# A hybrid decoder layer on one core: VectorE order in W_down, weight parts kept in DRAM, transpose banks, an early norm and one split moved

## The chip, the cores and the metric

The kernel runs on one core of one Trainium2 chip. The metric is the time of one execution on the device in microseconds. A profiled execution is slower or faster than the timed ones by some tenths of a per cent; where times inside an execution are compared, they come from the profiled one.

## What is computed

The layer takes x (1, 1024, 1024) in float32. Cut to what matters:

```python
h = rms_norm(x, norm_mix_pre)
proj = h @ w_in                                   # 1024 x 2568: u, v, z, xBC, dt
u_a, v_a, z_b, xbc_b, dt_b = split(proj)
y_a = gmlp_mixer(u_a, v_a, ...)                   # gelu, layer norm of v, causal 128 x 128 mixing per head
y_b = mamba2_mixer(z_b, xbc_b, dt_b, ...)         # conv of 4 taps, silu, chunked scan, silu gate, group norm
x = x + rms_norm(concat(y_a, y_b) @ w_out, norm_mix_post)
h = rms_norm(x, norm_ffn_pre)
f = square(relu(h @ w_up))                        # 1024 x 4096
x = x + rms_norm(f @ w_down, norm_ffn_post)       # 4096 x 1024
```

## The kernel before

Every large product is made of three matmuls on float32 operands that are split into a high part, rounded by a cast on ScalarE, and a low part, the difference (`split`, `split_psum`, `mm3`). The difference is taken on GpSimd for most weights and on VectorE where the operand lies in PSUM or the caller says so.

The tokens go through in two halves of 512 (H0, H1), each in four tiles of 128 tokens. `hT` holds the normed, transposed half as a pair `hTh`, `hTl`. Weights of w_in and w_out come in units of 128 x 1024 numbers (512 KB). `units` lists them in the order of use: 24 for H0 and the first product of W_out, then the same w_in units again for H1 with the second half of W_out's units between them, then units of w_up. `load_unit` loads a unit into one of two staging buffers (`ws`), casts `wh`, subtracts for `wl`, and `keep` stores both parts to DRAM if the unit comes again. `again` then loads both parts from there instead of splitting once more. There are five buffers each for `wh` and `wl`. Loads, stores and reloads are all issued on SP's queue.

The prologue (`PRO_OPS`) norms and transposes the first half: S is a sum of squares on ScalarE, R the reciprocal root on VectorE, N and M the product with the norm weight on VectorE or GpSimd, T the transposes, H and L the two parts of `hT`, W and V the cast and the difference of the first two units. For it the order of ScalarE, VectorE and GpSimd is held as written (`held = True` adds an order dependency from each instruction to the one before). Elsewhere the order of each engine comes from the framework's list scheduler, which works from its own model of time and from priorities in program order; TensorE's order is held as written for the up-projection (`pe.held`), VectorE's for the last output tiles.

PSUM has four `mm` banks, two `ss` banks for the state-space part and two `mi` banks. In H0 the last w_in product is `psu`; between its tiles `x1_tile` loads a tile of the second half of x (the load stands behind unit 15 and the following), norms it, transposes it in two `mm` banks and writes `hT` for H1. Behind it stand the spatial gating (`pssp`, `psya`) and W_out's first product (`pso`), which uses the four `mm` banks. `gate_norm` takes the group norm of the state-space output: `psgn`, a reciprocal root of four columns on VectorE (`rr`), `psgr`. `h2_tile` does for the up-projection what `x1_tile` does for H1.

The up-projection and W_down use a scheme of Winograd's with seven products in place of eight. In W_down a group of blocks has seven products (ORD: 1, 5, 6, 3, 7, 2, 4); each needs an f piece (cast on ScalarE, difference on GpSimd) and a weight piece (`w_block`: for products 5, 6, 7 and 4 a sum or difference `wt` on VectorE first; then a cast on ScalarE and a difference `wld` on VectorE). `preps[m + 2]` is written ahead of product m. `flush` adds a finished bank set (`pd`, four banks of the eight) into one of four accumulators `acc` on VectorE; the first use of an accumulator is a copy on ScalarE. The first group stands alone, so each of its products is flushed; the following three rounds take two groups at once and flush each second product. Product 3 is the first one whose flush is an add. The blocks left over are multiplied plainly at the end (`last_prep`, `pl`).

Of the kernel before, what the change touches and what calls it, by code (L numbers as in the profile page):

```python
# [8 lines left out]
F32 = mybir.dt.float32  # L9
# [32 lines left out]
N_TG = 6  # L42
TG_AFTER = (0, 1, 3, 5)
N_GROUP = N_PAIR // 2
X1_AFTER = 15
GM_AFTER = 4

PRO_LOADS = "0w1a23b"  # L50
PRO_BANK = (0, 0, 1, 2)
PRO_OPS = ("S0 R0 S1 W0 N0 R1 T0 H00 N1 V0 S2 H01 L00 S3 L01 T1 H10 L10 M2 H11 R23 W1 V1 L11 N3 C2 "
           "T2 T3 H20 H21 L21 H31 H30 L20 L30 L31 X")


# [1 line left out]
def hymba_kernel(ctx, tc, x, norm_mix_pre, w_in, gm_ln_w, gm_ln_b, gm_w_s, gm_b_s,  # L57
# [54 lines left out]
    def f(ap):  # L112
        return ap.bitcast(F32)
# [52 lines left out]
    def row_rstd(ss, n, base=None):  # L166
        steps = rstd_steps(ss, n, base)
        r = next(steps)
        for _ in steps:
            pass  # L170
        return r
# [64 lines left out]
    def keep(i):  # L236

        if any(u is units[i] for u in units[i + 1:]):
            parts[i] = [dram.tile([P, 1024], F32, name=f"wd{i}{j}") for j in range(2)]
            for d, t_ in zip(parts[i], ready[i]):  # L240
                nc.sync.dma_start(d, f(t_.rearrange("p a b -> p (a b)")))

    def again(i):
        shape = [P, 8, P] if units[i][0] == "m" else [P, 2, 512]
        hl = [wpool.tile(shape, F32R, tag=t_, bufs=N_SPLIT, name=f"{t_}{i}") for t_ in ("wh", "wl")]
        for d, t_ in zip(parts[first[id(units[i])]], hl):
            ins = nc.sync.dma_start(f(t_.rearrange("p a b -> p (a b)")), d)
        loads.append(ins.ins.name)
        ready.append(tuple(hl))

    def next_unit(ahead=2, eng=None):
        i = state["use"]
# [13 lines left out]
    def load_tok(src, name, unit=None):  # L266
        t = now["tok"].tile([P, D], F32, tag="tok", bufs=4, name=name)
        d = nc.sync.dma_start(t, src)
        if unit is not None:
            after(d, unit)  # L270
        return t
# [23 lines left out]
    def sumsq(src, name, ss=None):  # L295
        if ss is None:
            ss = const.tile([P, 1], F32, tag="ss", bufs=8, name=name)
        junk = now["tok"].tile([P, src.shape[-1]], BF16, tag="junk", bufs=1, name=f"{name}j")
        act.activation(junk, src, AF.Square, accum_out=ss)
        return ss  # L300

    def norm_transpose(xx, r, w, hT, t, name, bank):
        dve.scalar_tensor_tensor(xx, xx, r, w, op0=ALU.mult, op1=ALU.mult)
        transpose_split(xx, hT, t, name, bank)
# [10 lines left out]
    hT_tag = "hTh", "hTl"  # L315
    hT = tuple(hpool.tile([P, KB, HALF], F32R, tag=t_, bufs=1, name=t_) for t_ in hT_tag)

    def x1_tile(t):
        xx = load_tok(x[0, HALF + t * P:HALF + (t + 1) * P, :], f"x1_{t}", X1_AFTER + t)
        norm_transpose(xx, row_rstd(sumsq(xx, f"ssx1{t}"), D), wpre, hT, t, f"tx1{t}", mm_bank)  # L320

    mctx = stack()
    mpool = pool_of(mctx, "mpool")
# [43 lines left out]
    def step(op):  # L367
        kind, arg = op[0], op[1:]
        t = int(arg[0]) if arg else 0
        if kind == "S":  # L370
            ssx[t] = sumsq(x0[t], f"ssx0{t}")
        elif kind == "R":
            chains = [rstd_steps(ssx[int(c)], D) for c in arg]
            for c, steps in zip(arg, chains):
                rx[int(c)] = next(steps)
            while chains:
                chains = [c for c in chains if next(c, 0) is None]
        elif kind == "N":
            dve.scalar_tensor_tensor(x0[t], x0[t], rx[t], wpre, op0=ALU.mult, op1=ALU.mult)
        elif kind == "M":  # L380
            for q in range(2):
                qs = slice(q * 512, (q + 1) * 512)
                pool.tensor_tensor(x0[t][:, qs], x0[t][:, qs], wpre[:, qs], op=ALU.mult)
        elif kind == "C":
            act.activation(x0[t], x0[t], AF.Copy, scale=rx[t])
        elif kind == "T":
            for q in range(2):
                ps = (mm_bank, ss_bank, mi_bank)[PRO_BANK[t]](f"tx0{t}_{q}")
                psx[t, q] = ps.rearrange("p (k c) -> p k c", c=P)
                for k in range(4):  # L390
                    c0 = (4 * q + k) * P
                    pe.transpose(psx[t, q][:, k, :], x0[t][:, c0:c0 + P], ident)
        elif kind in "HL":
            q = int(arg[1])
            h, l = [y[:, 4 * q:4 * q + 4, t * P:(t + 1) * P] for y in hT]
            if kind == "H":
                act.copy(h, psx[t, q])
            else:
                dve.tensor_tensor(l, psx[t, q], f(h), op=ALU.subtract)
        elif kind == "W":  # L400
            st, shape = staged.pop(t)
            wh = wpool.tile(shape, F32R, tag="wh", bufs=N_SPLIT, name=f"wh{t}")
            wl = wpool.tile(shape, F32R, tag="wl", bufs=N_SPLIT, name=f"wl{t}")
            act.copy(wh, st)
            units01[t] = wh, wl, st
        elif kind == "V":
            wh, wl, st = units01[t]
            pool.tensor_tensor(wl, st, f(wh), op=ALU.subtract)
            ready.append((wh, wl))
            first[id(units[t])] = t  # L410
            keep(t)
            state["load"] += 1
        else:
            small_setup()
# [12 lines left out]
    def gm_setup():  # L427
        lnw = mpool.tile([P, GW], F32, name="lnw")
        lnb = mpool.tile([P, GW], F32, name="lnb")
        after(nc.sync.dma_start(lnw, gm_ln_w[0].rearrange("h p -> (h p)").partition_broadcast(P)), GM_AFTER)  # L430
        after(nc.sync.dma_start(lnb, gm_ln_b[0].rearrange("h p -> (h p)").partition_broadcast(P)), GM_AFTER)
        ws = mpool.tile([P, NH, P], F32, name="ws_t")
        for q in range(2):
            wst = s2("zt", f"wst{q}", shape=[P, 4, P], bufs=4)
            nc.sync.dma_start(wst, gm_w_s[0, 4 * q:4 * q + 4].rearrange("h t s -> t h s"))
            pool.affine_select(wst, wst, pattern=[[0, 4], [-1, P]], compare_op=ALU.is_ge,
                               fill=0.0, base=0, channel_multiplier=1)
            ps = mi_bank(f"wsT{q}")
            pv = ps.rearrange("p (k c) -> p k c", c=P)
            for k in range(4):  # L440
                pe.transpose(pv[:, k, :], wst[:, k, :], ident)
            act.copy(ws[:, 4 * q:4 * q + 4, :], pv)
        gm.update(lnw=lnw, lnb=lnb, ws=ws)
# [345 lines left out]
        conv_block(H0, key)  # L789
    group_prep(H0, 0)  # L790
    ssd_group(H0, 0)
    for key in XB[4:8]:
        conv_block(H0, key)
    gm_setup()
    group_prep(H0, 1)
    ssd_group(H0, 1)
# [43 lines left out]

    def h2_tile(t):
        xx = load_tok(h2d[t * P:(t + 1) * P, :], f"h2r{t}")
        transpose_split(xx, hT, t, f"tf{t}", mm_bank)

    H1.u = tok_dense_gelu(H1, "u", dense_tok_outer, lambda t: t and h2_tile(t - 1))
    h2_tile(3)
# [367 lines left out]
    def flush(i, ps):  # L1214
# [3 lines left out]
        else:  # L1218
            act.copy(a_, ps)
            done.add(INTO[i])  # L1220

    w_load(0, 0)
    floads[0]()
    w_load(0, 1)
# [147 lines left out]
```

## Time and profile before

| | us |
|---|---|
| median of 3 runs | 1070.66 |
| lowest and highest | 1070.23, 1070.66 |
| the profiled execution | 1074.9 |
| its span, first to last instruction | 1073.1 |

The profile is read from the page (busy time of each engine, its groups of like instructions), the list of waits, the timeline of one engine, tables of stretches with the granted clock of TensorE, and the list of DMA issues. PE is TensorE, DVE VectorE, ACT ScalarE, POOL GpSimd, and SPq the queue of SyncE that issues DMAs. Line 73 is the helper that records every operation, so the groups are told apart by tiles (out<-in). Matmuls are pipelined: one is written as 0.39 us, the next begins 0.23 us after it.

### The profile page before, as it was taken

How to read it: one execution, taken by the hardware profiler on the slowest of the kernel's cores; microseconds unless marked ns; L12 is line 12 of the kernel's file. 1: busy time of each engine (PE TensorE's matmuls, PEld its weight loads, DVE VectorE, ACT ScalarE, POOL GpSimd, SP SyncE). 2: the span in 40 equal slices, each digit the busy share in tenths (PEclk: the TensorE clock that was granted, in tenths of full speed). 3: DMA queues.
4: the chain of work that ended last, by engine and by line, in shares of the span. 5: the costliest groups of instructions: out<-in, count | busy, mean ns of one | idle time of the engine just before them, and what ended most of it. 6: DMA issues, size and time to landing. Idle time of an engine off the chain costs nothing. (4 is left out here: it accounts for less than half of the span.)

```text
span 1073.1 us, 13234 instructions
## 1 busy us (share of the span) xinstructions
PE 1023.7 (95%) x4735; PEld 836.4 (78%) x4735; DVE 743.8 (69%) x1265; ACT 468.6 (44%) x642; POOL 313.3 (29%) x169
## 2 busy tenths in 40 slices
PE   5989998999999999999999999999699999999996
PEld 4777776777788888888788888787588888888885
DVE  5647978366954835677477777775976777776677
ACT  5547443244343423675444444445533333333421
POOL 4454332030001002400111111112734444444533
PEclk9999898999999999999999999999989999999998
DMA  8997745475974263766756677766842552443422
GB/s 267 313 320 279 259 172 196 137 247 185 389 269 165 97 223 121 229 195 200 249 194 219 230 235 235 228 215 238 309 157 98 177 177 84 145 152 136 145 84 98
DMA packets 138857, 216.46 MB, mean 202 GB/s; under 512 B 9652, under 2 KB 72232, under 8 KB 138792
## 3 DMA queue, kind: packets, MB, share of 16 engines
q1 hardware_dynamic: 104360, 196.74, 53.1%
q10 hardware_dynamic: 34432, 18.88, 6.0%
q8 instruction: 37, 0.61, 0.2%
q14 instruction: 28, 0.23, 0.1%
HBM read 143.73 MB, written 71.86 MB: 201 GB/s over the span
## 5 line engine op out<-in xcount | busy, mean ns | idle before, releaser
L73 PE MATMUL pd<-whd,f 128*128 128x512 f32 x752 | 234.2, 392 | 7.9 <-DVE acc L73 7.9
L73 PEld LDWEIGHTS pd<-whd,f 128*128 128x128 f32 x752 | 142.3, 189 | 38.2 <-DVE acc L73 8.4
L73 POOL TENSOR_TENSOR f<-fr,f 128x1024 fp32r<-128x1024 f32 x47 | 118.5, 2524 | 147.2 <-ACT f L73 147.2
L73 PE MATMUL pd<-wld,f 128*128 128x512 f32 x376 | 147.4, 392 | 0.8 <-DVE wld L73 0.8
L73 POOL TENSOR_TENSOR wl<-ws,wh 128x1024 fp32r<-128x1024 f32 x36 | 87.7, 2440 | 191.9 <-ACT wh L73 191.7
L73 ACT CAST f<-fr 128x1024 fp32r<-128x1024 f32 x47 | 49.4, 1053 | 146.2 <-issue 132.2
L73 POOL TENSOR_TENSOR wlb<-sa,whb 128x1024 fp32r<-128x1024 f32 x16 | 38.5, 2407 | 225.1 <-ACT whb L73 213.9
L73 PEld LDWEIGHTS pd<-wld,f 128*128 128x128 f32 x376 | 71.3, 190 | 16.1 <-DVE wld L73 1.2
L73 DVE TENSOR_TENSOR wld<-wt,whd 128x1024 fp32r<-128x1024 f32 x28 | 63.5, 2267 | 26.9 <-ACT whd L73 26.9
L73 ACT ACTIVATE u<-u 128x512 f32<-128x512 f32 (+1 forms) x66 | 44.3, 672 | 61.6 <-DVE u L73 55.7
L73 ACT CAST wh<-ws 128x1024 fp32r<-128x1024 f32 x44 | 46.1, 1049 | 53.1 <-DMA ws<-in_w_in_dram 17.5
L73 DVE TENSOR_TENSOR acc<-pd,acc 128x2048 f32<-128x2048 f32 x24 | 54.9, 2287 | 14.8 <-PE pd L73 14.8
L73 DVE TENSOR_TENSOR wld<-wr,whd 128x1024 fp32r<-128x1024 f32 x21 | 47.8, 2276 | 22.8 <-ACT whd L73 22.8
L73 ACT ACT_TABLE_LOAD x30 | 38.5, 1283 | 27.9 <-DVE gg L73 8.7
L73 PE MATMUL pe<-hTh,wh 128*128 128x512 f32 x128 | 50.3, 393 | 0.0
L73 PE MATMUL pe<-hTh,wl 128*128 128x512 f32 x128 | 49.9, 390 | 0.0
L73 PE MATMUL pe<-hTl,wh 128*128 128x512 f32 x128 | 49.9, 390 | 0.0
L73 DVE TENSOR_TENSOR u<-puB,s 128x512 f32<-128x512 f32 x32 | 22.1, 692 | 31.6 <-DMA s<-early 15.8
L73 DVE TENSOR_SCALAR gg<-gg,acs 128x128 f32<-128x128 f32 x64 | 21.4, 396 | 19.9 <-DMA gg<-acd 19.9
L73 PE MATMUL pso<-wh,mixbh 128*128 128x512 f32 x64 | 28.0, 438 | 6.6 <-DVE hTl L73 5.3
L73 DVE TENSOR_TENSOR wlc<-sa,whc 128x1024 fp32r<-128x1024 f32 x16 | 29.2, 1824 | 5.6 <-ACT whc L73 5.6
L73 ACT CAST whd<-wt 128x1024 fp32r<-128x1024 f32 x28 | 29.3, 1046 | 5.7 <-DVE wt L73 2.8
(342 smaller groups left out, 2652.2 us busy)
## 6 DMA issues: line engine op xcount, KB each, us to landing
fr<-fsp SPq DMA_DIRECT2D x49, 512.0 KB, 3.8
wu<-in_w_up_dram ACTq DMA_DIRECT2D x32, 512.0 KB, 5.1
wr<-in_w_down_dram SPq DMA_DIRECT2D x32, 512.0 KB, 5.5
wd<-wh SPq DMA_DIRECT2D x28, 512.0 KB, 4.0
wd<-wl SPq DMA_DIRECT2D x28, 512.0 KB, 5.2
wh<-wd SPq DMA_DIRECT2D x28, 512.0 KB, 4.6
wl<-wd SPq DMA_DIRECT2D x28, 512.0 KB, 4.2
fsp<-c SPq DMA_DIRECT2D x42, 256.0 KB, 2.1
```

Source lines behind the costliest of these rows:

```text
L73: ins = fn(*a, **k)
```

## The change

Five edits.

1. VectorE's order is held as written from W_down's first instruction on (`dve.held = True` ahead of the first `w_load`).
2. `keep` stores the low part alone. `again` loads the unit's weights once more from the input into a staging buffer, loads `wl` from DRAM and casts `wh` on ScalarE.
3. `x1_tile` and `h2_tile` transpose in the `ss` banks.
4. The norm of the second half of x is taken out of `x1_tile` into `x1_norm`, which is written behind the four conv blocks of H0's second group; the loads stand behind units 5 to 8 instead of 15 to 18.
5. The first unit's difference (V0) goes from GpSimd to VectorE, and stands behind L00 in the prologue's order.

```diff
@@ -42,14 +42,14 @@
 N_TG = 6
 TG_AFTER = (0, 1, 3, 5)
 N_GROUP = N_PAIR // 2
-X1_AFTER = 15
+X1_AFTER = 5
 GM_AFTER = 4
 
 
 
 PRO_LOADS = "0w1a23b"
 PRO_BANK = (0, 0, 1, 2)
-PRO_OPS = ("S0 R0 S1 W0 N0 R1 T0 H00 N1 V0 S2 H01 L00 S3 L01 T1 H10 L10 M2 H11 R23 W1 V1 L11 N3 C2 "
+PRO_OPS = ("S0 R0 S1 W0 N0 R1 T0 H00 N1 S2 H01 L00 V0 S3 L01 T1 H10 L10 M2 H11 R23 W1 V1 L11 N3 C2 "
            "T2 T3 H20 H21 L21 H31 H30 L20 L30 L31 X")
 
 
@@ -236,17 +236,17 @@
     def keep(i):
 
         if any(u is units[i] for u in units[i + 1:]):
-            parts[i] = [dram.tile([P, 1024], F32, name=f"wd{i}{j}") for j in range(2)]
-            for d, t_ in zip(parts[i], ready[i]):
-                nc.sync.dma_start(d, f(t_.rearrange("p a b -> p (a b)")))
+            parts[i] = dram.tile([P, 1024], F32, name=f"wd{i}")
+            nc.sync.dma_start(parts[i], f(ready[i][1].rearrange("p a b -> p (a b)")))
 
     def again(i):
-        shape = [P, 8, P] if units[i][0] == "m" else [P, 2, 512]
-        hl = [wpool.tile(shape, F32R, tag=t_, bufs=N_SPLIT, name=f"{t_}{i}") for t_ in ("wh", "wl")]
-        for d, t_ in zip(parts[first[id(units[i])]], hl):
-            ins = nc.sync.dma_start(f(t_.rearrange("p a b -> p (a b)")), d)
-        loads.append(ins.ins.name)
-        ready.append(tuple(hl))
+        if i not in staged:
+            stage_unit(i)
+        st, shape = staged.pop(i)
+        wh, wl = [wpool.tile(shape, F32R, tag=t_, bufs=N_SPLIT, name=f"{t_}{i}") for t_ in ("wh", "wl")]
+        nc.sync.dma_start(f(wl.rearrange("p a b -> p (a b)")), parts[first[id(units[i])]])
+        act.copy(wh, st)
+        ready.append((wh, wl))
 
     def next_unit(ahead=2, eng=None):
         i = state["use"]
@@ -315,9 +315,15 @@
     hT_tag = "hTh", "hTl"
     hT = tuple(hpool.tile([P, KB, HALF], F32R, tag=t_, bufs=1, name=t_) for t_ in hT_tag)
 
+    x1 = {}
+
+    def x1_norm(t):
+        xx = x1[t] = load_tok(x[0, HALF + t * P:HALF + (t + 1) * P, :], f"x1_{t}", X1_AFTER + t)
+        r = row_rstd(sumsq(xx, f"ssx1{t}"), D)
+        dve.scalar_tensor_tensor(xx, xx, r, wpre, op0=ALU.mult, op1=ALU.mult)
+
     def x1_tile(t):
-        xx = load_tok(x[0, HALF + t * P:HALF + (t + 1) * P, :], f"x1_{t}", X1_AFTER + t)
-        norm_transpose(xx, row_rstd(sumsq(xx, f"ssx1{t}"), D), wpre, hT, t, f"tx1{t}", mm_bank)
+        transpose_split(x1[t], hT, t, f"tx1{t}", ss_bank)
 
     mctx = stack()
     mpool = pool_of(mctx, "mpool")
@@ -405,7 +411,7 @@
             units01[t] = wh, wl, st
         elif kind == "V":
             wh, wl, st = units01[t]
-            pool.tensor_tensor(wl, st, f(wh), op=ALU.subtract)
+            (pool if t else dve).tensor_tensor(wl, st, f(wh), op=ALU.subtract)
             ready.append((wh, wl))
             first[id(units[t])] = t
             keep(t)
@@ -789,8 +795,9 @@
         conv_block(H0, key)
     group_prep(H0, 0)
     ssd_group(H0, 0)
-    for key in XB[4:8]:
+    for t, key in enumerate(XB[4:8]):
         conv_block(H0, key)
+        x1_norm(t)
     gm_setup()
     group_prep(H0, 1)
     ssd_group(H0, 1)
@@ -840,7 +847,7 @@
 
     def h2_tile(t):
         xx = load_tok(h2d[t * P:(t + 1) * P, :], f"h2r{t}")
-        transpose_split(xx, hT, t, f"tf{t}", mm_bank)
+        transpose_split(xx, hT, t, f"tf{t}", ss_bank)
 
     H1.u = tok_dense_gelu(H1, "u", dense_tok_outer, lambda t: t and h2_tile(t - 1))
     h2_tile(3)
@@ -1219,6 +1226,7 @@
             act.copy(a_, ps)
             done.add(INTO[i])
 
+    dve.held = True
     w_load(0, 0)
     floads[0]()
     w_load(0, 1)
```

## Rows read from the trace of the kernel before

**Rows 1.** The page, busy time (share of the span) and instructions of each engine

```profile
PE 1023.7 (95%) x4735; PEld 836.4 (78%) x4735; DVE 743.8 (69%) x1265; ACT 468.6 (44%) x642; POOL 313.3 (29%) x169
```

**Rows 2.** Waits, whole span: us in total, times, longest us

```profile
ACT wh L73 <- DMA ws<-in_w_in_dram: 17.5, 7, 5.1
...
PE tx L73 <- DVE x L73: 12.0, 2, 8.9
...
PE pd L73 <- DVE acc L73: 7.9, 1, 7.9
...
PE pso L73 <- DVE hTl L73: 5.3, 2, 4.0
...
PE psC L73 <- DVE gg L73: 3.3, 1, 3.3
...
PE psgr L73 <- DVE rr L73: 2.7, 1, 2.7
```

**Rows 3.** Four stretches: PE, PEld, DVE, ACT, POOL busy; PEclk; DMA, GB/s

```profile
80.40:83.60 3.20, 3.20 (x9) 2.54 (x8) 3.10 (x8) 2.63 (x5) 2.54 (x2) 0.50 0.83 310
128.20:134.80 6.60, 6.11 (x18) 5.20 (x19) 6.39 (x18) 1.24 (x2) 1.56 (x3) 0.50 0.51 122
179.40:186.00 6.60, 5.29 (x13) 3.63 (x13) 4.17 (x12) 0.00 (x0) 1.33 (x1) 0.50 0.92 345
773.30:783.40 10.10, 5.55 (x13) 4.39 (x14) 10.06 (x6) 0.00 (x0) 4.51 (x2) 0.50 0.42 136
```

**Rows 4.** Timeline of VectorE, 758 to 780 us: start, us, operation

```profile
761.10 1.21 DVE L73 TENSOR_TENSOR wld<-wr,whd 128x1024 fp32r<-128x1024 f32 x1
762.23 3.42 DVE L73 TENSOR_TENSOR wld<-wt,whd 128x1024 fp32r<-128x1024 f32 x1
765.58 3.43 DVE L73 TENSOR_TENSOR wt<-wr,wt 128x1024 f32<-128x1024 f32 x1
...
775.52 2.28 DVE L73 TENSOR_TENSOR acc<-pd,acc 128x2048 f32<-128x2048 f32 x1
```

**Rows 5.** Timeline of GpSimd, 740 to 800 us

```profile
761.07 16.74 POOL L73 TENSOR_TENSOR f<-fr,f 128x1024 fp32r<-128x1024 f32 x5 [4.39 <-ACT f L73]
```

**Rows 6.** VectorE by form, 800 to 1000 us: busy us, mean ns | idle before

```profile
L73 DVE TENSOR_TENSOR wld<-wt,whd 128x1024 fp32r<-128x1024 f32 x21 | 50.4, 2398 | 19.6 <-ACT whd L73 19.6
L73 DVE TENSOR_TENSOR acc<-pd,acc 128x2048 f32<-128x2048 f32 x19 | 43.5, 2287 | 10.1 <-PE pd L73 10.1
L73 DVE TENSOR_TENSOR wld<-wr,whd 128x1024 fp32r<-128x1024 f32 x16 | 37.4, 2335 | 22.8 <-ACT whd L73 22.8
```

**Rows 7.** The page's costliest groups: the casts of weights on ScalarE

```profile
L73 ACT CAST wh<-ws 128x1024 fp32r<-128x1024 f32 x44 | 46.1, 1049 | 53.1 <-DMA ws<-in_w_in_dram 17.5
```

**Rows 8.** Timeline of TensorE, 168 to 192 us

```profile
178.66 0.50 PE L73 MATMUL pso<-wh,mixbh 128*128 128x512 f32 x1 [3.95 <-DVE hTl L73]
```

**Rows 9.** Timeline of VectorE, 172 to 184 us

```profile
183.59 0.15 DVE L73 SCALAR_TENSOR_TENSOR rr<-rt,rr 128x4 f32<-128x4 f32 x1
```

**Rows 10.** Timeline of VectorE, 117 to 129 us

```profile
122.41 1.28 DVE L73 SCALAR_TENSOR_TENSOR x<-x,rr,wpre 128x1024 f32<-128x1024 f32 x1
...
126.21 2.23 DVE L73 TENSOR_TENSOR rt<-rt,rr 128x4 f32<-128x4 f32 x1
```

**Rows 11.** DMA issues: engine, count, KB each, median us to landing

```profile
wh<-wd SPq DMA_DIRECT2D x28, 512.0 KB, 4.6
...
ws<-in_w_in_dram SPq DMA_DIRECT2D x20, 512.0 KB, 6.6
```

**Rows 12.** Timeline of SP's queue, 60 to 80 us

```profile
68.98 0.32 SPq L241 DMA_DIRECT2D wd<-wh  x1
69.42 1.29 SPq L606 DMA_DIRECT2D gg<-acd  x2
```

**Rows 13.** The tile `wh`, 255 to 300 us, loads from DRAM

```profile
DMA to landing us min/median/max: 5.5/8.1/9.2
```

**Rows 14.** Timeline of VectorE, 8 to 26 us

```profile
11.26 2.62 DVE L73 SCALAR_TENSOR_TENSOR x<-x,rr,wpre 128x1024 f32<-128x1024 f32 x1
```

## The prediction

> **What bounds the kernel now.** I read the page's busy times first: TensorE is busy for 95% of the span and no other engine for more than 69% [rows 1]. So the reader has to look for what is not matmul: TensorE's waits, and the stretches at its lower clock behind them. The list of waits gives five of TensorE's that matter here [rows 2]: 12.0 us in the prologue, 7.9 us in W_down on VectorE's add into an accumulator, 5.3 us where W_out's first product of the first half waits for VectorE's `hTl`, 3.3 us on the first decay tile and 2.7 us on the group norm's reciprocal root. Behind the last four the granted clock is 0.50, that is 1.2 instead of 2.4 GHz, for a stretch [rows 3]. Matmul time in such a stretch counts half: 3.20 us lose 1.6, 6.11 lose 3.1, 5.29 lose 2.6, 5.55 lose 2.8. So a wait has two prices: W_down 7.9 + 2.8 = 10.7 us, W_out 5.3 + 2.6 = 7.9, decay 3.3 + 1.6 = 4.9, norm 2.7 + 3.1 = 5.8. Everything else that the change moves lies beside a busy TensorE.
>
> **1. VectorE's order in W_down.** The timeline shows what the scheduler's own order did [rows 4]: the add of product 3 (`acc`) ran at 775.52, and four preparations for later products stood in front of it. Each would take 1.21 us, but took 3.4 us, since GpSimd ran five operations back to back over the same stretch [rows 5]. So the order put 4 x 3.4 us before an add for which TensorE was waiting. Program order puts the add right behind the split of piece 2 (b21). The add ended at 777.8, so TensorE had stopped 7.9 us before, at 769.9, one product (5.4 us: 37 splits, one for each product, in 200 us [rows 6]) after product 3, which was ready by 764.5; the split of b21 ends at 762.3 [rows 4], so the add runs at 764.5 to 766.8 and TensorE goes on at 769.9 without a stall. Next late is product 4: t4 and its split, one cast between them, then the add of product 7. Alone these take 1.2 + 1.05 + 1.2 + 2.3, so TensorE stalls 0 to 0.8 us; with each operation on SBUF at 3.4 us, 1.7 us there and up to 5 us by the second group's t1. I take 1.5, near the lower end, because a VectorE that waits lets GpSimd finish meanwhile: **-10.7 + 1.5 = -9.2 us**.
> In the steady part a pair of products with sums now needs one add, two sums, two casts and two splits in a row: 2.3 + 2 x (1.2 + 1.05 + 2.4) = 11.6 us against 10.8 us of TensorE [rows 6, 7]. Pairs without sums need 2.3 + 2 x 2.3 = 6.9. Four of seven pairs have sums, so a round has 7 x 10.8 = 75.6 us for 67.1 of work, and the lag of at most two pairs in succession (1.6 us) lies inside the lead of two products: 0.
> At the end the last two pieces of the remainder are split behind the last add instead of before it: 2.3 + 1.2 + 1.2 = 4.7 us, against 6 matmuls (1.4 us) of the first output tile that need neither. If TensorE takes the same 6 matmuls of the other three tiles whose banks are free, that is covered; if it keeps tile order, it waits 3 us and loses up to 3 to the clock. I take **+1.0** of 0 to 6.
>
> **2. Transposes in the state-space banks.** `x1_tile` no longer takes two of the four `mm` banks, for which W_out's product waited [rows 8]; the `ss` pair holds only the last state-space tiles by then. The 24 matmuls then run from 174.7 (178.66 less the wait of 3.95) to 180.1. Next late is the group norm's root, written at 183.7 [rows 9], so up to 3.6 us of the gain wait there; spatial gating's matmuls can fill some. Bounds 0 (the wait moves to the `ss` pair, whose reader is the same VectorE) and -7.9; I take 2.0 us left over: **-5.9**. For `tf` in the second half no wait is listed: 0.
>
> **3. x's second half normed early.** The four chains (each 9 short operations, some 1.9 us, and 1.28 us for the product) move out of the stretch where the other norm's root was interleaved with them [rows 10]; one of its short steps also took 2.23 us under a GpSimd operation, and that may stay. Bounds 0 and -5.8; I take half: **-3.0**. The loads of x move from units 15 to 18 to units 5 to 8 on SP's queue, 4 x 512 KB into the busiest stretch of DMA; each meets the one 512 KB store of `wh` that part 4 takes away there. About 13 us of VectorE's work now stand earlier among conv and decay operations. Every change of this kind also lets the scheduler sort the whole first half anew: 0 to two stalls like the norm's (11.6); I take half of one: **+3.0**.
>
> **4. Low parts alone in DRAM.** Gone are 28 stores of `wh` and 28 reloads [rows 11]; added are 28 reloads of the raw weights into the two staging buffers and 28 casts of 1.05 us on ScalarE [rows 7], which is busy 44% [rows 1]. Bytes read stay the same, 14.7 MB of stores go. On SP's queue one store less stands ahead of each load: the decay tile's load was issued at 69.42 right behind such a store at 68.98 [rows 12], but it also needs the landing of `acd`. Bounds: 1.3 us lost (one product of part 3 in front of the decay's first operation) and -4.9; I take a third: **-1.5**. In the second half a cast now stands in ScalarE's order and waits for its load, which lands in 6.6 us (`wh` from DRAM 4.6) [rows 11]. In the first half such casts waited 17.5 us in 7 instances [rows 2], and the list of TensorE's waits has none on a cast. In the stretch from 255 to 300 us a load of `wh` took up to 9.2 us [rows 13]; at that landing two buffers give a unit every (9.2 + 1.05 + 2.5)/2 = 6.4 us (2.5 = 17.5/7) against 5.4, so the eight units there could cost 8 us. Bounds 0 and 8; I take **+2.0**.
>
> **5. First W split on VectorE.** The second norm product took 2.62 us beside GpSimd's split, where the same operation takes 1.28 [rows 10, 14]. Transposes wait for it, so -1.3; the split itself (1.2 to 2.6 us) now stands on VectorE before three `hTl` splits. Bounds -2.6 (also the next 1.2 us transposes' wait) and +1.3; **-1.0**. What bears on this is the Trainium skill, SBUF — State Buffer, section Who interferes with whom: a VectorE instruction with two SBUF inputs and a GpSimd instruction that reads SBUF exclude one another, and issue order decides who waits. The splits at 1.21 and 3.4 us agree [rows 4], and the adds from PSUM stay at 2.29 us [rows 6]. Perfetto Trace Analysis of the Trainium skill, section Optimizing Scalar/DVE Operations, warns that moving work between these two engines might not help; by it this part gives 0, the sum 1.0 less.
>
> **Sum.** -9.2 + 1.0 - 5.9 - 3.0 + 3.0 - 1.5 + 2.0 - 1.0 = -14.6 us. The profiled execution took 1074.9 us with a span of 1073.1; its terms are shifts of the same program, so I take them off the median, 1070.66: **1056.1 us**.
>
> **Rivals.** *A. Only W_down gains.* The wait of part 2 moves to the `ss` pair or to the root, and the first half gives as much as it takes: -9.2 + 1.0 + 2.0 gives 1064.5. For it: the same VectorE ends these waits; against: two of them end on a bank or on work that the change takes away. 20%. *B. VectorE in order becomes the bound of W_down.* If the two products of lead are used up, each of four pairs with sums in three rounds costs 0.8 to 1.1 us, 13 at most: 1069.3. Against it: 67.1 of 75.6 us. 7%. *C, slower: casts behind late loads.* Place: the second half, where none of the five waits lies. If ScalarE waits as in the first half and all 28 raw loads land in 9.2 us, a unit comes 0.95 us late, 26.6 us in all: 1056.1 - 2 + 26.6 = 1080.7. It decides from about 18 late units, or from a landing plus wait above 9.8 us throughout. For it: ScalarE's silu, exp and evacuations stand behind the casts; against: DMA is full in that stretch only from 255 to 300 us. 11%. The Trainium skill, Perfetto Trace Analysis, section DMA Optimizations, says that small DMAs, under 2 KB, have a marked cost for each transfer; a block of w_in is read in 512-byte rows, and the 6.6 against 4.6 us of landing agree [rows 11]. *D. The change does not do what it says:* the waits of W_down stay, since ScalarE's order, which is free, holds them; the rest as summed: 1065.3. 2%.
>
> **How the numbers follow.** The forecast with its parts, 1044 to 1063, has 60%; it is the likeliest, so 1056.1 stands. With A and D it reaches 1066; with half of B to 1069. All parts at their best would be 1039, which I leave out with C. Range **1044 to 1069**. A measurement of this kernel can tell about 0.2% (2.1 us). Faster: 60 + 20 + 2 + 1 of B = 83%; same: 6% of B; slower: C, 11%.
>
> **What would show it.** In W_down the adds follow the split of b21, none waits behind three preparations, and TensorE's 7.9 us on `acc` is under 2, with no stretch at 0.50. W_out starts within 1 us of the last `psu`; the first `psgr` does not wait; no DRAM tile for `wh`. Wrong would be: idle TensorE between 200 and 430 us with ScalarE's casts waiting on `ws`, a wait on `wld` every round after 800 us, a stall at the first `pl` tile, or a new wait between 60 and 130 us behind x's chains.

## The result, and the profile after

The changed kernel takes 1057.08 us (median of 4 runs, 1054.97 to 1058.54) against 1070.49 us for the kernel before: a ratio of 0.9873, with a 95% interval from 0.9855 to 0.9892. The forecast was 1056.1 us. A second set of runs gave 1055.47 us and 0.9853 (0.9821 to 0.9885). So the time came out where it was forecast; the sum behind it did not come out term by term, as the experiments show. (A ratio is taken from the single runs, none of which was in the slow state, and not from the two medians; the two can differ by some tenths of a per cent.)

First the page of the kernel after (busy time, share of the span, instructions), which answers to [rows 1]: in a span of 1055.9 us TensorE is busy for 97%; ScalarE has 27 us more, the casts of the second half.

```profile
PE 1019.6 (97%) x4735; PEld 833.9 (79%) x4735; DVE 756.4 (72%) x1266; ACT 495.4 (47%) x670; POOL 313.3 (30%) x168
```

Then TensorE's waits in the kernel after (us in total, times, longest), which answer to [rows 2]. The waits for `acc` in W_down, for `gg`, for the first group's root and W_out's for `hTl` are gone. The two longest new ones are 3.8 us for `da`, the last step of the dt chain, and 2.4 us in which transposes of x wait for `hTl`, the reader of the state-space pair; the other new ones are 1.5 us or less.

```profile
PE psa L73 <- DVE da L73: 3.8, 1, 3.8
...
PE tx L73 <- DVE hTl L73: 2.4, 1, 2.4
...
PE pl L73 <- DVE acc L73: 0.8, 1, 0.8
```

The two stretches at half clock that are left among the products of the kernel after (columns as in [rows 3]) stand at just these two waits:

```profile
66.30:73.00 6.70, 5.81 (x16) 4.75 (x17) 3.37 (x14) 0.54 (x3) 0.62 (x2) 0.50 0.68 191
178.90:182.30 3.40, 3.40 (x14) 2.93 (x13) 3.05 (x6) 0.36 (x1) 0.00 (x0) 0.50 0.94 267
```

How long such a stretch lasts, and whether it comes at all, differs between executions. In the profile of the second set the same two waits stand (3.8 and 2.3 us), but at `da` the stretch is 3.4 us long instead of 6.8, one of 3.4 us stands at 234.9 us, and behind the transposes' wait, which ends at 175.1 us there, the granted clock stays at 1.00:

```profile
175.20:178.60 3.40, 3.39 (x24) 2.81 (x24) 2.77 (x6) 1.38 (x3) 0.00 (x0) 1.00 0.55 122
```

Where the time went between the two profiled executions (span 1073.1 to 1055.9 us, 17.2 less), read from the first instruction of each stage: the first half with W_out gained 6.6 us by the last product of W_out (262.0 against 268.6 us), the second half gave back 1.4 (first product of the next stage at 422.2 against 427.4), the up-projection gained 2.1, W_down 10.8, and the remainder behind it lost 1.1. The medians differ by 13.4, not 17.2, so some 4 us of the profiled pair are scatter. The 2.1 of the up-projection appear in kernels with quite different edits too (1.7 to 2.4 us with three of the five edits made alone, 0.4 and 0.5 with the other two), so I put them down to none.

The timeline of VectorE in the kernel after at the start of W_down, which answers to [rows 4]: the add of product 3 runs at 757.11, with one sum behind it, and none of the preparations of later products in front.

```profile
752.78 1.22 DVE L73 TENSOR_TENSOR wld<-wr,whd 128x1024 fp32r<-128x1024 f32 x1
757.11 2.29 DVE L73 TENSOR_TENSOR acc<-pd,acc 128x2048 f32<-128x2048 f32 x1 [3.11 <-ACT f L73]
759.32 2.77 DVE L73 TENSOR_TENSOR wt<-wr,wt 128x1024 f32<-128x1024 f32 x1
```

### The profile page after: what moved, and what is told of

Read it like the earlier page. It is cut to its first block, busy times and chain, and to the rows that moved or that the text cites. A ratio compares the mean times of both kernels' runs of the same rounds, so it can differ in the third digit from the quotient of the medians.

```text
span 1055.9 us, 13181 instructions
## 1 busy us (share of the span) xinstructions
PE 1019.6 (97%) x4735; PEld 833.9 (79%) x4735; DVE 756.4 (72%) x1266; ACT 495.4 (47%) x670; POOL 313.3 (30%) x168
## 4 chain that ended last, share of the span: by engine, by line
PE 82%; DVE 8%; DMA 5%; ACT 3%; issue 1%; DVEq 0%; ACTq 0%; SPq 0%
PE pd L73 25%; PE pe L73 8%; PE puC L73 8%; PE puB L73 8%; PE pso L73 6%; PE puD L73 4%; PE psz L73 4%; PE pl L73 4%; PE psv L73 4%; DMA ws<-in_w_in_dram 2%; PE psu L73 2%; PE psB L73 2%; PE psx L73 1%; PE psC L73 1%; DVE v L73 1%
## 5 line engine op out<-in xcount | busy, mean ns | idle before, releaser
L73 POOL TENSOR_TENSOR wl<-ws,wh 128x1024 fp32r<-128x1024 f32 x35 | 85.2, 2437 | 166.2 <-ACT wh L73 163.2
L73 ACT CAST wh<-ws 128x1024 fp32r<-128x1024 f32 x72 | 75.3, 1048 | 92.1 <-DMA ws<-in_w_in_dram 20.9
L73 DVE TENSOR_TENSOR wld<-wt,whd 128x1024 fp32r<-128x1024 f32 x28 | 36.7, 1310 | 35.2 <-ACT whd L73 34.0
L73 DVE TENSOR_TENSOR wld<-wr,whd 128x1024 fp32r<-128x1024 f32 x21 | 60.0, 2888 | 0.8 <-ACT whd L73 0.8
L73 DVE TENSOR_TENSOR wt<-wr,wt 128x1024 f32<-128x1024 f32 x14 | 35.9, 2561 | 0.0
L73 ACT ACTIVATE f<-f 128x512 f32<-128x512 f32 x32 | 20.2, 632 | 29.6 <-DVE f L73 29.1
```

The costliest lines, as they stand in the source:

```text
L73: ins = fn(*a, **k)
```

## The experiments

Each of the five parts of the change was made alone on the kernel before; the order and the early norm were also taken out of the changed kernel, and three further kernels are new. The expectations number the parts as edits: 1 the order in W_down, 2 the low parts, 3 the banks, 4 the early norm, 5 the first split. The prediction's steps have another numbering, so the text goes by names.

**The order alone, and all but the order.** The line that holds VectorE to program order is put into the kernel before, or taken out of the changed one.

```diff
+    dve.held = True
     w_load(0, 0)
     floads[0]()
```

> The kernel before with edit 1 alone (VectorE's order held from W_down on). Theory: the 7.9 us wait on the add of product 3 and the half-clock stretch behind it are due to VectorE's order alone, and the last pieces behind the last add cost about 1 us: W_down's products 10 to 11 us shorter, no wait above 1 us in them, 1060 to 1061.5 us in all. Rival: the wait went because the first half was sorted anew and W_down's loads and casts came at other times; then the wait stays and the time is 1069 to 1071.

> The changed kernel without edit 1. Theory: W_down waits again, 6 to 8 us on an add and some us at half clock, so 1057.1 + 9.7 = 1066.8 us, with the first 730 us as in the changed kernel. Rival (the order is not what took the wait away): 1056 to 1058 and no wait above 1 us in W_down.

Measured: 1062.86 us alone, ratio 0.9918 (0.9894 to 0.9942), that is 8.8 us less (6.2 to 11.4); without it 1066.61 us, ratio 0.9946 (0.9926 to 0.9966), 5.8 us less. 8.8 and 5.8 make 14.6, and the whole change is 13.4 or, in the second set, 16 us: within these intervals the price of the order does not depend on the rest. TensorE's waits with the order alone show why. The 7.9 us on `acc` are gone, and the waits of the first half stand as in [rows 2]:

```profile
PE pso L73 <- DVE hTl L73: 5.0, 2, 4.0
PE psC L73 <- DVE gg L73: 3.4, 1, 3.4
...
PE psgr L73 <- DVE rr L73: 2.8, 1, 2.8
```

The wait for `gg` ends at 78.7 us here, and no half-clock stretch follows it, although it is as long as in the kernel before:

```profile
78.00:86.00 8.00, 7.28 (x45) 5.66 (x45) 6.04 (x17) 5.30 (x8) 2.98 (x2) 1.00 0.89 322
```

With the order taken out, the same list has the old line back:

```profile
PE pd L73 <- DVE acc L73: 7.9, 1, 7.9
```

**Last pieces ahead of the last add.** The two splits that held order puts behind the last add of W_down are moved in front of it.

```diff
+        if m + 1 == len(seq):
+            for j in range(len(seq) + 2, len(preps)):
+                ...
+                preps[j]()
         if g == gs[-1]:
             flush(i, ps)
-    for m in range(len(seq) + 2, len(preps)):
-        ...
-        preps[m]()
```

> The changed kernel with the last two pieces of the remainder written ahead of the last add. Theory: the 0.8 us wait at the first output tile is due to their place behind that add, so it goes: 1056.3 us, 0.8 less. Rival: TensorE's banks wait for the add itself, not for the pieces: no wait is saved, 1057 us.

Measured: 1057.60 us, ratio 0.9865 (0.984 to 0.989), no different from the changed kernel. The theory fell. TensorE still waits for the add, 1.0 us instead of 0.8, since four splits in a row now stand in front of it; the timeline of VectorE in this kernel shows them:

```profile
993.66 7.63 DVE L73 TENSOR_TENSOR wldl<-wr,whdl 128x1024 fp32r<-128x1024 f32 x4
1001.22 2.28 DVE L73 TENSOR_TENSOR acc<-pd,acc 128x2048 f32<-128x2048 f32 x1
```

**The low parts alone.** On the kernel before, `keep` stores only the low part and `again` casts the high part anew.

```diff
-        for d, t_ in zip(parts[i], ready[i]):
-            nc.sync.dma_start(d, f(t_.rearrange("p a b -> p (a b)")))
+        nc.sync.dma_start(parts[i], f(ready[i][1].rearrange("p a b -> p (a b)")))
...
+        act.copy(wh, st)
```

> Edit 2 alone on the kernel before: only the low part of W_in is kept in DRAM, the high part is loaded and cast again in the second half. The prediction's step 4 says -1.5 us (half of the 3.3 us wait of psC for gg) and +2.0 us (casts in the second half), so 1071.0 us, within 1070.0 to 1072.5; the gg wait stays at 1 to 2 us and the second half has casts that TensorE waits for. Rival: the 29 MB less to write free the queue in front of gg altogether and the casts of the second half cost nothing, the gg wait is gone with its half-clock stretch: 1066 to 1068 us. Second rival: the casts land late in the second half, 1073 us or more.

Measured: 1069.56 us, ratio 0.9973 (0.9954 to 0.9992), 2.9 us less (0.9 to 4.9). The prediction had +0.5 for this edit. (The stores that go are 28 of 512 KB, 14.7 MB, and not the 29 MB of the expectation.) The waits of TensorE in this kernel, against [rows 2]: the wait for `gg` fell from 3.3 to 1.4, as the theory had it, but the root's wait fell from 2.7 to 0.4 and W_out's from 5.3 to 2.9, which no step of mine had put here.

```profile
PE pso L73 <- DVE hTl L73: 2.9, 1, 2.9
...
PE psC L73 <- DVE gg L73: 1.4, 1, 1.4
...
PE psgr L73 <- DVE rr L73: 0.4, 1, 0.4
```

The stretch from 60 to 110 us (columns as in [rows 3]) shows what changed there: first the kernel with the order alone, which stores both parts, then this one.

```profile
60.00:110.00 50.00, 46.56 (x243) 37.50 (x241) 30.15 (x77) 31.01 (x41) 22.64 (x15) 1.00 0.90 316
```

```profile
60.00:110.00 50.00, 46.74 (x240) 36.62 (x239) 28.78 (x79) 29.71 (x42) 19.94 (x14) 1.00 0.57 190
```

DMA is busy 0.90 of it where both parts are stored, and 0.57 where one is (0.90 and 0.76 from 10 to 60 us).

**The early norm alone.** The transposes stay in the matmul banks.

```diff
-X1_AFTER = 15
+X1_AFTER = 5
...
-    for key in XB[4:8]:
+    for t, key in enumerate(XB[4:8]):
         conv_block(H0, key)
+        x1_norm(t)
```

> Edit 4 alone on the kernel before: x's second half is loaded and normed between the convolutions of the first half, its transposes stay where they were, in the matmul banks. The prediction's step 3 says -3.0 us for the root that TensorE waits for at 126 us and +3.0 for the work re-sorted at 45 to 65 us: 1070.5 us, within 1069 to 1072; the wait of psgr for rr is gone and a wait of psa for da (the dt chain, 3.8 us in the changed kernel, with a half-clock stretch) has come. Rival: the dt chain has slack without the other edits, so only the gain is left: 1066 to 1068 us and no wait for da. Second rival: the wait for da comes and the wait for rr stays, since the norms were not what held the root: 1074 us or more.

Measured: median 1075.97 us, ratio 1.0021 (1.0000 to 1.0043), 0 to 4.6 us slower. Of the expected marks both came: the first group's root no longer waits, and TensorE waits 2.8 us ahead of the dt chain's first product (the list names `rr`, which VectorE wrote beside `da`). W_out's first product still waits, 5.0 us, and the root that waits 2.4 us is now the second group's, at 190 us.

```profile
PE pso L73 <- DVE hTl L73: 5.0, 1, 5.0
...
PE psa L73 <- DVE rr L73: 2.8, 1, 2.8
PE psgr L73 <- DVE rr L73: 2.4, 1, 2.4
```

The row of `da` in this kernel (duration min/median/max in ns, first and last start in us) has its first start at 63.8 us; with any one of the other four parts it is 54.6 to 57.4 us.

```profile
L73 DVE TENSOR_TENSOR da<-dt,aneg x2: 185/189/193, 63.8 to 237.5; 128x32 f32<-128x32 f32 x2
```

**The banks alone.** Both groups of transposes go to the state-space pair.

```diff
-        norm_transpose(xx, row_rstd(...), wpre, hT, t, f"tx1{t}", mm_bank)
+        norm_transpose(xx, row_rstd(...), wpre, hT, t, f"tx1{t}", ss_bank)
...
-        transpose_split(xx, hT, t, f"tf{t}", mm_bank)
+        transpose_split(xx, hT, t, f"tf{t}", ss_bank)
```

> Edit 3 alone on the kernel before: the transposes of x's second half and of h2 use the state-space bank pair. The prediction's step 2 says -7.9 +2.0 = -5.9 us: 1064.6 us, within 1063 to 1067; the two waits of pso for hTl (5.3 us together) are gone and their half-clock stretch with them, and a wait of at most 2.4 us of the last transpose for the pair stands in their place. Rival: the copies of the last block are late on VectorE whatever the bank, so that the transposes of the pair wait about as long as pso did: 1069 to 1071 us.

Measured: 1068.91 us, ratio 0.9963 (0.9943 to 0.9983), 4.0 us less (1.8 to 6.1); the theory's 1064.6 lies outside. (Its profiled execution, at 1072.94 us, was one of its longest; W_down's wait for `acc` is 9.3 us in it instead of 7.9.) The mechanism is as forecast: `pso` no longer waits for `hTl`, and the transposes wait for the pair instead, 1.9 us:

```profile
PE psC L73 <- DVE gg L73: 3.7, 1, 3.7
...
PE tx L73 <- DVE hTl L73: 1.9, 1, 1.9
```

**The first split alone.** It is made on VectorE, and `V0` moves behind `L00` in the order of the start.

```diff
-            pool.tensor_tensor(wl, st, f(wh), op=ALU.subtract)
+            (pool if t else dve).tensor_tensor(wl, st, f(wh), op=ALU.subtract)
```

> Edit 5 alone on the kernel before: the low part of the first W unit is made on VectorE instead of GpSimd, a few places later in the order of the start. The prediction's step 5 says -1.0 us: 1069.5 us, within 1069 to 1070.5; the first convolution matmul starts about 1.2 us earlier, as in the changed kernel (14.55 us against 15.73), and part of this lasts to the end. Rival: what starts earlier waits again for the next unit or for the dt chain by 60 us, so that nothing is left: 1070.5 us, with the z block starting at 80.3 us as before.

Measured: 1068.55 us, ratio 0.9963 (0.9943 to 0.9982), 4.0 us less (1.9 to 6.1), four times the 1.0 of the prediction. The first convolution product starts at 14.31 us against 15.73, but the second waits 1.0 us for `rv`, and the first product of the dt chain comes at 57.6 us against 56.8: by then the lead is used up. The gain came at 75 us: the wait for `gg` is gone, and a z product that waits 2.4 us for `carry` has taken its place, without the half-clock stretch behind it. The split's engine and its place in the order were changed together, and no run separates them. The Trainium skill, Perfetto Trace Analysis, section Optimizing Scalar/DVE Operations, warns that moving work between these two engines might not help. Here, alone, it helped: 4.0 us.

**All but the early norm, twice.** The early norm is taken out of the changed kernel and the state-space banks are kept. Only in the second set did it run beside the changed kernel.

```diff
-X1_AFTER = 5
+X1_AFTER = 15
...
-    for t, key in enumerate(XB[4:8]):
+    for key in XB[4:8]:
         conv_block(H0, key)
-        x1_norm(t)
```

> The changed kernel with edit 4 undone (x's second half normed behind the u product again, its transposes in the ss banks). Theory: the early norm takes the wait on the group norm's root away (2.7 us and 3.1 by the clock) and puts one on the dt chain instead (3.8 us and up to 3.4 by the clock), so the two cancel: 1054 to 1058 us, the wait on da gone, one on the root back. Rival: the early norm is where the first half gains, as its root's wait does not come back otherwise: 1060 to 1063.

> The changed kernel without edit 4 (x's second half is loaded, normed and transposed as before, in the state-space banks), beside the changed kernel on one chip. Theory: edit 4 costs, it doesn't gain: the norms of x stand on VectorE among the steps of the dt chain and push da from 51-57 us to 64-67 us, behind the work that covers it, while the root that it was to free is late for another reason; 2 to 3 us below the changed kernel, 1053 to 1056 us, da at about 51 us, no half-clock stretch at 66 us. Rival (the prediction's step 3): gain and re-sorting cancel, within 1 us of the changed kernel, and the 2 us seen between the two before were scatter.

> The changed kernel itself again, as the measure for the other three of this set: 1055 to 1058 us, with the wait of psa for da (3.8 us at 63 us), da made at 66 to 67 us, and a half-clock stretch behind it.

Measured: 1055.12 us (ratio 0.9844, 0.9819 to 0.9869), then 1054.25 us beside 1055.47 us of the changed kernel. From the logarithms of the six runs each of that set, the kernel without the early norm stands at 0.9990 of the changed one (0.9978 to 1.0002). So it is not slower, and perhaps 1 us faster: less than the theory's 2 to 3 us, and the rival's cancelling within 1 us can't be ruled out. The places are clear, though. `da` starts at 51.0 us instead of 65.9 beside it and 67.0 in the first set, TensorE's wait for it is 1.1 instead of 3.8 us, the transposes' wait is off the list, the first group's root, which was to need the early norm, has no wait, and the second group's has 1.2 us. The waits of TensorE in the second of these runs:

```profile
PE psgr L73 <- DVE rr L73: 1.2, 1, 1.2
PE psa L73 <- DVE da L73: 1.1, 1, 1.1
```

**The early norm written behind the dt chain.** The loads stay early; the norms move from the loop of the convolutions to that of the z blocks.

```diff
-        x1_norm(t)
     gm_setup()
...
     for b in range(4):
         z_block(H0, b)
+        x1_norm(b)
```

> The changed kernel with the norms of x's second half moved from the loop of the convolutions to the loop of the four z blocks, behind the dt chain and the first decay steps; loads due as early as in the changed kernel. Theory: what costs is the place (norm steps in between the steps of the dt chain), not the early norm: da is back at 51 to 57 us, the wait of psa for da is under 1 us, and the time is 1053 to 1056 us, at or below the kernel without edit 4. Rival: VectorE has no slack in the z blocks either, so the waits of TensorE for gg, carry or the root grow by what the wait for da gave up: 1056 to 1059 us.

Measured: 1052.20 us, ratio 0.983 (0.9799 to 0.9861) to the kernel before and 0.9978 (0.9962 to 0.9994) to the changed kernel of the same set: 2.3 us faster than that one, and so faster than both kernels of the pair. Against the kernel without the early norm it is at 0.9988 (0.9969 to 1.0007), which settles nothing. The time is as expected, but the mark did not come: `da` starts at 62.5 us, not at 51 to 57. The lines were moved and the work was not, since VectorE's order here is the scheduler's: three of the four norm products still run ahead of `da`, as the groups of VectorE's instructions from 38 to 62.5 us show. So this kernel does not test the theory of the place. What is less is the chain's meetings with GpSimd: its seven like steps (`q__0_387`) take 3.2 us instead of 7.6 in the changed kernel, while `dt` takes 2.2, and the wait is half.

```profile
PE tx L73 <- DVE hTl L73: 2.4, 1, 2.4
...
PE psa L73 <- DVE da L73: 1.9, 1, 1.9
```

```profile
L73 DVE SCALAR_TENSOR_TENSOR x<-x,rr,wpre 128x1024 f32<-128x1024 f32 x3 | 3.8, 1282 | 0.0
```

**Order, banks and first split, without the low parts and the early norm.** From the kernel without the early norm it differs by the low parts only: both parts are stored and reloaded as before.

```diff
+        parts[i] = [dram.tile([P, 1024], F32, name=f"wd{i}{j}") for j in range(2)]
+        for d, t_ in zip(parts[i], ready[i]):
+            nc.sync.dma_start(d, f(t_.rearrange("p a b -> p (a b)")))
...
-        act.copy(wh, st)
```

> The kernel before with edits 1, 3 and 5 alone: neither the low parts (edit 2) nor the early norm (edit 4). Theory: edits 2 and 5 free the same wait, that of psC for gg at 75 us, so that beside edit 5 edit 2 has nothing left to gain: within 1 us of the kernel without edit 4 alone, 1053.5 to 1057 us, and the gg wait under 1 us although both parts are written to DRAM and loaded again. Rival: edit 2 keeps the 2.9 us that it gained alone: 1057 to 1060 us, with a gg wait above 1 us or casts and loads that TensorE waits for.

Measured: 1061.82 us against 1054.25 with the low parts: 1.0070 (1.0054 to 1.0087), or 7.4 us. The theory, that the low parts and the first split free the same wait and no more, fell, and the 2.9 us of its rival were too few. The waits of TensorE in this kernel: that for `gg` is gone, as the theory said, but the transposes wait 5.2 us, the root 2.3 and a state product 2.0.

```profile
PE tx L73 <- DVE hTl L73: 5.2, 2, 4.2
PE psgr L73 <- DVE rr L73: 2.3, 1, 2.3
PE psB L73 <- DVE cbm L73: 2.0, 1, 2.0
```

The loss has one place. At W_out's first product the profiled kernel is 9.1 us ahead of the kernel before (169.59 against 178.66 us [rows 8]), so up to there the banks and the first split keep their gain; at its last product of the first half it is 0.7 ahead (267.5 against 268.2), where the one with the low parts is 11.0 ahead at both. The first and the last product, and the half-clock stretch between them:

```profile
169.59 0.40 PE L73 MATMUL pso<-wh,mixbh 128*128 128x512 f32 x1
```

```profile
L73 PE MATMUL pso<-wh,mixal x32: 388/394/479, 200.6 to 267.5; 128*128 128x512 f32 x32
```

```profile
181.70:188.50 6.80, 5.62 (x23) 4.35 (x20) 5.23 (x12) 2.25 (x4) 0.73 (x1) 0.50 0.99 327
```

The transposes' 5.2 us and half of these 5.62 are 8.0 of the 8.4 lost. The longest wait can be followed back. On ScalarE, in the timeline of this kernel, the copies of the last transposes (`hTh<-tx`) stand behind a cast that waited 6.63 us for a load of W_out:

```profile
170.41 1.92 ACT L73 ACTIVATE u<-u 128x2048 f32<-128x2048 f32 x1
178.96 1.04 ACT L73 CAST wh<-ws 128x1024 fp32r<-128x1024 f32 x1 [6.63 <-DMA ws<-in_w_out_dram]
179.91 1.07 ACT L73 CAST hTh<-tx 128x512 fp32r<-128x512 f32 x2
```

That load was issued on SP at 173.01, behind stores of `wl` and `wh`, and the first of these had waited for GpSimd's split, which took 6.17 us from 165.93, beside a row of VectorE's products; the median of such splits in the kernel before is 2.4. (The first line below has this split, the longer of two.) From the cast the chain runs over `hTh` and `hTl` to the 4.19 us of TensorE that end at 181.27. The queue of SP in the same kernel comes second:

```profile
L73 POOL TENSOR_TENSOR wl<-ws,wh x2: 2832/4502/6173, 165.9 to 172.1; 128x1024 fp32r<-128x1024 f32 x2
```

```profile
172.13 0.32 SPq L241 DMA_DIRECT2D wd<-wl  x1
172.54 0.38 SPq L241 DMA_DIRECT2D wd<-wh  x1
173.01 0.67 SPq L213 DMA_DIRECT2D ws<-in_w_out_dram  x1
```

Where only the low parts are stored, SP's queue has the load at 167.92, right behind the store of `wl` of a split that took 2.58 us, and ScalarE waits 0.29 us for it:

```profile
167.92 0.38 SPq L213 DMA_DIRECT2D ws<-in_w_out_dram  x1
```

So the cast comes 7.06 us later where both parts are stored (178.96 against 171.90): 1.0 by the later start of the split, 3.6 by its length, 0.5 by the second store on the queue and 2.0 by the load itself (5.95 us from issue to cast against 3.98). Only the last two can be put down to the added stores; why the split met VectorE's products so much longer was not traced.

The raw loads of `ws` between 10 and 190 us, first with both parts stored, then with the low ones alone (issue to landing, us, min/median/max):

```profile
DMA to landing us min/median/max: 4.1/6.3/9.0
```

```profile
DMA to landing us min/median/max: 4.0/4.7/6.5
```

## Why the prediction was right, and where it was not

**The time and the side were right, by steps of which some were wrong and made up for one another.** Forecast -14.6 us, measured -13.4 and, in the second set, -16.

**Step 1, W_down: right, in mechanism and size.** Forecast -9.2, and +1.0 behind the last add; sum -8.2; measured -8.8 alone. The stall on `acc` went wholly, where 1.5 us were put down as left. TensorE waits 0.8 us for the last add, and the 1.0 us taken for the tail came out at 1.1. (The prediction saw the wait at the first `pl` tile as a sign against it; it came, 0.8 us long.) That held order would not become the bound (rival B) is right too: between 770 and 1000 us VectorE was busy 195 of 230 us instead of 171, and TensorE had no wait there. One thing turned that the steps had not: the splits from `wt` fell from a mean of 2398 ns [rows 6] to 1276, and those from `wr` rose from 2335 to 3221.

```profile
L73 DVE TENSOR_TENSOR wld<-wr,whd 128x1024 fp32r<-128x1024 f32 x16 | 50.9, 3221 | 0.0
...
L73 DVE TENSOR_TENSOR wld<-wt,whd 128x1024 fp32r<-128x1024 f32 x20 | 25.5, 1276 | 22.4 <-ACT whd L73 22.4
```

**Step 2, the banks: right in mechanism, too large.** Forecast -7.9 + 2.0; measured 4.0 less alone. The rest moved to the pair, 1.9 us alone and 2.4 with the other edits, and not to the root, for which I had left the 2.0. The mis-sized term is the 2.0: it should hold the wait and its clock price. In the kernel with the banks alone that is 1.9 us and 3.4 us at 0.50, which is 1.7, so 3.6, and in the changed kernel 2.4 + 1.7 = 4.1; -7.9 + 3.6 to 4.1 is about what the banks alone measured. The price by the clock is not certain, though, as the prediction's sums take it: in the second set's profile the same wait has no such stretch behind it, and with the order alone the wait for `gg` has none. In the kernel after the lateness is again a short step beside GpSimd: ahead of the last `hTl` a root step of 128x4 takes 2.23 us, where its neighbours take 0.16, as in [rows 10].

```profile
173.24 2.23 DVE L73 TENSOR_TENSOR rt<-rv,rr 128x4 f32<-128x4 f32 x1
175.50 0.16 DVE L73 TENSOR_TENSOR rt<-rt,rr 128x4 f32<-128x4 f32 x1
```

**Step 3, the early norm: -3.0 and +3.0 cancelled on paper, 0 to +4.6 alone, about +1 (-0.2 to +2.3) in company.** With the edit alone the wait of the first group's root at 126 us goes, but the second group's waits 2.4 us in its place. The first group's is gone, or down to 0.4 us, in every kernel that stores the low parts alone, early norm or not, so beside the low parts this step had next to nothing left to win. The loss I had put into an unnamed re-sorting has a place: VectorE does the norms among the steps of the dt chain. The groups of VectorE's instructions in the kernel after, 38 to 66.9 us, where `da` starts (busy us, mean ns), and the first form without the early norm, 38 to 69 us:

```profile
L73 DVE SCALAR_TENSOR_TENSOR q__0_387<-q__0_387,z 128x32 f32<-128x32 f32 x7 | 7.6, 1084 | 0.0
L73 DVE SCALAR_TENSOR_TENSOR x<-x,rr,wpre 128x1024 f32<-128x1024 f32 x3 | 3.8, 1282 | 0.0
```

```profile
L73 DVE SCALAR_TENSOR_TENSOR q__0_387<-q__0_387,z 128x32 f32<-128x32 f32 x7 | 1.3, 190 | 0.2
```

Three of the four products stand ahead of `da`; they take 3.8 us and, with the norms' short steps, some 10 us. Seven steps of the dt chain take 7.6 us instead of 1.3, for three of them meet a split on GpSimd and take 2.2 to 2.4 us each: 6.3 us more. (One more step of the chain takes 2.3 us in either kernel, `ab` here and `zz` without the early norm.) Together some 16 us on the engine ahead of `da`, which started 16 us later (67.0 against 51.0); TensorE had slack for most of it and waited 3.8 us instead of 1.1. That the norms' place is the cause is read from this order, and no run shows it alone. The prediction named "a new wait between 60 and 130 us behind x's chains" as a sign against it. It stands at 63 us.

**Step 4, the low parts: wrong in sign.** Forecast -1.5 and +2.0; measured -2.9 alone and -7.4 beside the order, the banks and the first split. The step priced the stores by the one wait at 69 us behind which a store was seen [rows 12], and left aside that the 14.7 MB go from a stretch in which DMA is 0.9 busy. The loads of weights there land in 4.7 instead of 6.3 us (median), and waits shrink that the list puts down to VectorE: the root, the transposes, W_out. Most of the 7.4 us lies in the one stall of the transposes in W_out, and of the 7.1 us by which its cast is late some 2.5 can be put down to the stores (the second store on the queue and the load's slower landing), 4.6 to GpSimd's later and longer split. That full DMA is the cause is thus shown for a part of the price and argued for the rest. The price in the second half was +2.0 of 0 to 8; from the last product of W_out in the first half to the stage behind the second the profiles lose 1.4 us in the changed kernel and 0.6 with the low parts alone, and 0.3 in the combination that stores both. Rival C, the late casts of the second half, stayed away: between 255 and 300 us DMA was busy throughout and the raw loads took 8.3 us in the median, near the 9.2 of my bound, and yet TensorE was busy 44.78 of 45 us. Here is that stretch of the kernel after:

```profile
255.00:300.00 45.00, 44.78 (x227) 35.72 (x226) 41.98 (x142) 27.75 (x40) 3.07 (x5) 1.00 1.01 353
```

So the two buffers of the bound were not what paced the units there; what did give them their lead was not traced.

**Step 5, the first split: too small alone, and won elsewhere.** Forecast -1.0, bounds -2.6 and +1.3; measured -4.0 (-6.1 to -1.9). The first product comes 1.4 us earlier, about as forecast, but by the first product of the dt chain the kernel is 0.9 us behind. Between there and the first v product it gains 5.1: the `gg` wait and its clock price (4.9), which I had credited in part to the low parts, go, and 2.4 for `carry` come; the rest was not traced. That a split at 10 us would move a wait at 75 us was in no step.

**The parts do not add up.** Alone they sum to -8.8 - 4.0 + 2.3 - 2.9 - 4.0 = -17.4. Yet order, banks and first split together give 0.9911 (0.9881 to 0.9941), the order alone 0.9918 (0.9894 to 0.9942): banks and first split, 4.0 us each by themselves, add 0.8 us to the order, with some 4 us of uncertainty since the two kernels are of different sets, until the low parts join them. That the low parts are worth more there, 7.4 us against 2.9, is shown by the times. The gain of banks and split is not missing from the start: it is there up to W_out and goes in one stall. The chain above shows how (a split held up by VectorE, a store behind it, a load behind the store, a cast behind the load, and the transposes' copies behind the cast). For the root, and for the state product that waits 2.0 us, the link to the stores was not traced. Whether the transferred bytes or the stores' place on SP's queue matter more stays open: no run separates them, and in the stall above the place is 0.5 us and the slower load 2.0.

## What to carry to other kernels

Price a store not by the one instruction that is seen behind it but by all that stands behind it on its queue, and look how full DMA is in that stretch: at 0.9 busy, halving the stores of weights was worth 2.9 us alone and 7.4 in company, though none of TensorE's waits named a DMA, and in the 7.4 a split held up on GpSimd weighed more than the stores. Before moving work earlier on an in-order engine, look for the chain that it will stand among there; a step of 0.2 us in such a chain can cost 2.3 when it meets an operation on the neighbouring engine. And test edits in company as well as alone: stalls that end on the same engines can share their causes, and what two edits win can be lost again in one stall that a third, which looked cheapest, takes away. An edit of the program's order has moved work only where the engine's order follows it: read the new place from the trace.

## What the runs showed of the hardware that I had not expected

Short operations suffer most, for their size, beside GpSimd. In the kernel after, VectorE's step on 128x32 values took 2.39 us from 61.36 and the same form 0.19 at 63.78; GpSimd's split ran from 61.26 for 2.44 us. The two timelines:

```profile
61.36 2.39 DVE L73 SCALAR_TENSOR_TENSOR q__0_387<-q__0_387,z 128x32 f32<-128x32 f32 x1
...
63.78 0.19 DVE L73 SCALAR_TENSOR_TENSOR q__0_387<-q__0_387,z 128x32 f32<-128x32 f32 x1
```

```profile
61.26 2.44 POOL L73 TENSOR_TENSOR wl<-ws,wh 128x1024 fp32r<-128x1024 f32 x1 [3.33 <-ACT wh L73]
```

The rule of the Trainium skill, SBUF — State Buffer, section Who interferes with whom (a VectorE instruction with two SBUF inputs and a GpSimd instruction that reads SBUF exclude one another), agrees: the step ends within 0.05 us of the split. So in these rows the price is what is left of GpSimd's operation: 2.2 us more for a step of 0.19 us here, and likewise 3.4 instead of 1.2 us for the splits and sums of 128x1024 in [rows 4].
